# Leaving 384 bytes free under the left side's pools of a one-core hybrid block

## The chip, the cores and the metric

The kernel runs on one core of one Trainium2 chip, in one launch. The metric is the device time of an execution in microseconds (us). Before the change three executions took 1248.18, 1248.79 and 1250.2 us, so the median is 1248.79 us.

Engines are called PE (TensorE; PEld is its weight load), DVE (VectorE), ACT (ScalarE), POOL (GpSimd) and SP (SyncE, which issues most transfers).

## What is computed

One block of a hybrid encoder on x [1, 1024, 1024] in float32. Cut to what matters here:

```
h    = rms_norm(x, pre_mix_gain);  z, xbc, dt, q, k, v = split(h @ w_in)
y_ssd = group_norm(ssd(silu(conv(xbc)), dt) * silu(z))   # 8 heads, chunks
y_sb  = head_norm(stick_breaking_attention(q, k, v))     # 8 heads of 64
x1   = x + rms_norm(concat(y_ssd, y_sb) @ w_out, post_mix_gain)
h2   = rms_norm(x1, pre_ffn_gain)
out  = x1 + rms_norm((silu(h2 @ w_gate) * (h2 @ w_up)) @ w_down, post_ffn_gain)
```

d_model is 1024, the feed-forward width 2816 (22 tiles of 128).

## The kernel before

**Products.** Every large product is made of three: an operand is split into a high and a low part (`split`, L70 to L73: ACT makes the high part, DVE the rest), and `mm3` (L75 to L78) issues high times high, high times low, low times high into one PSUM bank. In a matmul the *stationary* operand (`lhsT`, 128x128 here) is loaded by PEld, and the *moving* operand (`rhs`, 128x512) streams past it. In the profile's names `pd<-folo,fohi` the first name behind the arrow is the moving operand, the second the stationary one; where one name stands, both are tiles of that name.

**Stages.** First in_proj, with attention and SSD interleaved beside it (matmuls `pj_*`, `zp`, `tp`, `o`, `py`), to about 480 us. Then out_proj and the two norms (`po`, `pt`), to about 640 us. Then gate and up as Winograd's seven products per pair of feed-forward tiles (`quad`: `pag`, `pau`, `pbg` .. `peu`): 11 pairs x 2 matrices x 7 products x 12 matmuls = 1848 matmuls of 128x512, to about 1031 us. Then down, again as seven products (`pd`, 924 matmuls), and the last norm.

**Where tiles lie.** On-chip memory (SBUF) is handed out from two ends. Pools with `side="left"` grow upward, pools with `side="right"` grow downward; a pool opened after another was closed takes its place. All addresses below are bytes per partition in the built program. Below the left pools lies `base`, with the identity `ident` (address 16512) and the packed small parameters `pk` (17024, 76 floats). Everything else on the left stands on top of that: `const`, then for the first half `stg`, `att`, `big`, `sml`, `t2`; for the second half `small_p`, `fwA`, `rpA`, `rpB`.

What matters below is where an operand starts within 2048 bytes, since each 128x512 float32 operand is 2048 bytes long, and a 128x128 one 512 bytes:

| operands | pool, side | address modulo 2048 before |
|---|---|---|
| in_proj: `hh`, `hl` moving, `wh_*`, `wl_*` stationary | `hp`, `wp`, right | 2016 (stationary slices at 2016 + 512 i) |
| attention: `kh`, `kl`, `wh`, `wl` moving, `qq`, `vv` stationary | `att`, left | 1984 (+ 512 i) |
| SSD and others in `t2` | left | 256 |
| out_proj: `woh`, `wol` moving | `wo`, right | 2016 |
| out_proj: `yhl` stationary, blocks 2 and 3 (in `rpA`'s places `T3h`, `T3l`, L764) | left | 1632 (+ 512 i) |
| out_proj: `yhl` stationary, the other blocks | `wo`, right | 2016 (+ 512 i) |
| gate and up: `B11`, `B21`, `T2`, `T3`, `T1`, `T4`, `B22` moving | `rpA`, `rpB`, left | 1632 |
| gate and up: first two products' stationary `eo` | `fwA`, left | 1632 (+ 512 i) |
| gate and up: all later stationary `flhi`, `fllo` (`pair`, L936) | `fw`, right | 2016 (+ 512 i) |
| down: `fohi`, `folo`, `doh`, `dol`, both operands | `fw`, `dp`, right | 2016 (+ 512 i) |

So in gate and up the moving operand lies on the left and the stationary one on the right, 384 bytes apart modulo 512; in down both lie on the right, no bytes apart modulo 512. 1848 - 48 = 1800 matmuls of gate and up have `flhi` or `fllo` as stationary operand.

**Order.** Instructions of an engine run in the order in which they stand. PE takes its products one after the other; `pump` and `LOOK` make the left operands of gate and up ahead of their use, `prep` and `AHEAD` those of down.

Of the kernel before, what the change touches and what calls it, by code (L numbers as in the profile page):

```python
# [8 lines left out]
F32 = mybir.dt.float32  # L9
# [4 lines left out]
PSUM = bass.MemoryType.PSUM  # L14
DRAM = bass.MemoryType.DRAM

P = 128
S = 1024
D = 1024
ND = D // P  # L20
NB = S // P
# [13 lines left out]
# what in_proj makes, in order; "ssd" from where on SSD's steps run beside the tiles  # L35
PLAN = ('qkv1', 'x0', 'x1', 'x2', 'x3', 'x4', 'x5', 'qkv2', 'x7', 'x6', 'ssd', 'qkv3', 'z0', 'z1', 'r0', 'z2', 'z3', 'wo', 'l1', 'o0')
# how far attention is where the other stream is 0, 1/8, .. 1 done
# [10 lines left out]
def tile_hybrid_block(  # L48
# [15 lines left out]
    """The rows of x and out run backwards in time (row s is token S-1-s), so that every  # L64
    running product over earlier tokens is a forward scan along the free axis."""
# [4 lines left out]
    def split(hi, lo, src):  # L70
        """hi + lo == src, hi and lo each exact in float32r."""
        A.copy(hi, src)  # L72
        V.tensor_tensor(lo, src, f32(hi), ALU.subtract)  # L73
# [6 lines left out]
    # ------------------------------------------------------------------ constants  # L80
# [11 lines left out]
    make_identity(nc, ident)  # L92
    pk = base.tile([P, 76], F32, name="pk")
# [7 lines left out]
    # TensorE's clock rises with use: products of ones while the first loads run  # L101
# [3 lines left out]
    # tri[s, l] = 1 where s >= l  # L105
    tri = const.tile([P, P], F32, name="tri")
    G.affine_select(tri, ones_f, [[-1, P]], ALU.is_ge, 0.0, base=0, channel_multiplier=1)
    # scan floor: 1 where the key is not strictly before the query, 0 elsewhere
# [3 lines left out]
    # column h is 1 on the 64 partitions of head h of a pair  # L112
# [11 lines left out]
    # DRAM scratch  # L124
# [5 lines left out]
    # means of squares and what they make 1 / rms: even heads, odd heads, SSD groups  # L130
# [8 lines left out]
    # ------------------------------------------------------------------ right side: x * gain and in_proj weights  # L139
# [4 lines left out]
    # the rows' 1 / rms scales columns here, so it is applied to what comes out of in_proj  # L144
# [13 lines left out]
    # sel16 sums the products of the two halves of w2  # L158
# [11 lines left out]
    # columns of w_in in the order of their use; each tile is loaded and split while the one before it  # L170
    # is multiplied
# [5 lines left out]
    def fetch_w(half=None):  # L177
        """The next column tile, or one half of it."""
        if cols:
            name, col = cols[0]  # L180
            w = w_tiles.setdefault(name, [])
            for dh in range(2) if half is None else (half,):
                w.append(load_w_half(col, name, dh))
            if len(w) == 2:
                cols.pop(0)
# [8 lines left out]
    # ------------------------------------------------------------------ pre-mix norm, first products  # L194
# [40 lines left out]
    # ------------------------------------------------------------------ left side: attention, conv and SSD work  # L235
# [20 lines left out]
    def qkv_tiles(j, st):  # L256
        """What takes q, k (each in its two parts) and v of a pair of heads out of PSUM, to DRAM."""

        def store(key, n, i, t):
            nc.sync.dma_start(qkv_d[j][key][i][:, 512 * n : 512 * n + 512], t)  # L260

        def two(key, n, src):
            hi, lo = [t2.tile([P, 512], F32R, tag="t2", name=key + x) for x in "hl"]
            split(hi, lo, src)
            store(key, n, 0, f32(hi))
            store(key, n, 1, f32(lo))

        def evac_q(n, ps, sl):
            two("q", n, ps)
            st["q"] = n == 1  # L270

        def evac_k(n, ps, sl):
            kr = t2.tile([P, 512], F32, tag="t2", name="kr")
            V.tensor_tensor(kr, ps, R_b[:, sl], ALU.mult)
            two("k", n, kr)
            st["k"] = n == 1

        def evac_v(n, ps, sl):
            vr = t2.tile([P, 512], F32, tag="t2", name="vr")
            V.tensor_tensor(vr, ps, R_b[:, sl], ALU.mult)  # L280
            if j == 0:
                v_first.append(vr)
            else:
                store("v", n, 0, vr)
            if n == 1:
                st["v"] = True

        return evac_q, evac_k, evac_v
# [7 lines left out]
    # ------------------------------------------------------------------ dt, decays  # L296
    def dt_stage():
# [18 lines left out]
        # softplus(x) = max(x, 0) + log1p(exp(-|x|)), log1p(e) = 2 atanh(e / (2 + e))  # L316
# [43 lines left out]
        # attention's sigmoids, which need these, wait for the last exponential: ScalarE changes its table once  # L360
# [4 lines left out]
    # ------------------------------------------------------------------ conv tiles  # L365
# [38 lines left out]
    # ------------------------------------------------------------------ SSD  # L404
# [76 lines left out]
    def mean_sq(src, sel, rows, n, cnt, ps=None, start=True, stop=True):  # L481
        """Means of squares over channels, to the rows of ss_d."""
# [32 lines left out]
    # ------------------------------------------------------------------ stick-breaking attention  # L515
    CH = {128: [128], 256: [256], 384: [384], 512: [512], 640: [384, 256], 768: [512, 256], 896: [512, 384], 1024: [512, 512]}

    def prep_head(j, st, h):
        """Keys over both halves of the partitions, the query's high part beside its low part."""
# [29 lines left out]
    def weigh(head, qb):  # L549
        """A key k weighs sigmoid(z_k) * prod_{q < i < k} sigmoid(-z_i)."""  # L550
# [20 lines left out]
    def turn(ws, g, jj):  # L571
        """Weights of 256 queries and 256 keys, keys to the partitions, split."""
# [27 lines left out]
    def attention(st):  # L600
        """All heads, as one stream of small steps: products with the values lag the transposes,
        the next queries' weights run ahead of them."""
# [53 lines left out]
    def merge(ga, gb):  # L656
        """Interleave attention with the other stream, as PACE has it."""
# [47 lines left out]
    # ------------------------------------------------------------------ out_proj: the products  # L705
    # position p of a block of 128 tokens: from here on the last rows come first
# [14 lines left out]
    # the channels in the order of their use: attention's first, the SSD's second group last  # L721
    KO = (4, 5, 6, 7, 0, 1, 2, 3)

    def fetch_wo():
        """W_out's rows in the order of their use, and the places of their two parts."""
# [31 lines left out]
    def out_load(p, part):  # L757
        """A block of the mixed channels, scaled by their 1 / rms, split: all but the SSD's second
        group, that group, or all."""
# [89 lines left out]
    # ------------------------------------------------------------------ out_proj, post-mix norm, residual, pre-ffn norm  # L849
    # positions 0 .. 7 of a block of 128 tokens: from here on the last rows come first  # L850
# [3 lines left out]
    def row_rstd(ssq):  # L854
        """-2 (ssq / D + eps) ** -0.5 for [P, 2] partial sums; the gains it multiplies take in the -1 / 2."""
# [15 lines left out]
    # Gate and up as the seven products of Winograd's form of Strassen's product: blocks of 512  # L871
    # tokens, halves of d, and pairs of tiles of f. h2 is the right operand:
    #   [b11 b12; b21 b22], halves of d by halves of the tokens
# [13 lines left out]
    def product(ps, lop, rop, start):  # L887
        """ps = or += the product; a bank that was read goes on accumulating after that."""
        (ah, al), (bh, bl) = lop, rop
        for k in range(4):  # L890
            mm3(ps, ah[:, k, :], al[:, k, :], bh[:, k, :], bl[:, k, :], start and k == 0, k == 3, not start)
# [4 lines left out]
    def quad(p, name):  # L896
        """The 2 x 2 blocks of W^T h from seven products. c11 is left in PSUM."""
# [35 lines left out]
    def left_gen():  # L933
        """The left operands in the order of their use, gate and up in turn."""
# [51 lines left out]
    def step(p):  # L986
        """The next product of gate's and of up's quad p."""
# [8 lines left out]
    def gate(t):  # L996
        """A block of a from gate's and up's."""
# [8 lines left out]
    # which block of a the products make  # L1006
    where = {1: (0, 0), 4: (1, 1), 5: (1, 0), 6: (0, 1)}

    with es_o:
# [3 lines left out]
        def early_ops():  # L1013
            """The left operands of the first two products."""
# [35 lines left out]
        def out_tail(sb, t):  # L1050
# [20 lines left out]
            # T3 = b22 - b12, T2 = T3 + b11, T1 = b12 - b11, T4 = b21 - T2: its product enters with that sign  # L1071
# [50 lines left out]
        # not the ring's next banks: those hold what waits for the last norm  # L1122
# [7 lines left out]
    # ------------------------------------------------------------------ gate and up  # L1130
# [12 lines left out]
    # Down as seven products too: halves of the tokens, even and odd tiles of f, halves of d.  # L1143
    #   a: [a11 a12; a21 a22], tokens by f; w: [b11 b12; b21 b22], f by d
    # What stays on chip takes the places of what gate and up no longer need, in this order.
# [35 lines left out]
    def prep(i):  # L1181
        """The operands of a step, a product's part of one pair of tiles of f."""
# [60 lines left out]
    # ------------------------------------------------------------------ down, post-ffn norm, residual  # L1243
    dp = ctx.enter_context(tc.tile_pool(reuse_waits="tile", name="dp", bufs=1, side="right"))
    gp_b = gain_b(dp, "gp_b", post_ffn_gain)
    ssq = dp.tile([P, NB, 2], F32, name="ssq")
# [12 lines left out]
    def finish(b, halves, xr):  # L1259
        """halves: the block's two, times the gain."""  # L1260
# [76 lines left out]
def _layout(inputs):  # L1337
    """x backwards in time, plain and transposed; the small parameters side by side, a channel
    (of its tile of 128) to a partition; the large ones as they are."""
# [32 lines left out]
```

## Time and profile before

One execution was profiled. The page gives its span, 1249.6 us from the first to the last instruction; its own time is not listed apart from that. The span lies within the three times that were measured (1248.18 to 1250.2 us).

| stretch, us | PE busy | DVE busy | mean DMA share | what runs |
|---|---|---|---|---|
| 0 to 480 | 457.08 | 388.72 | 0.49 | in_proj, attention, SSD |
| 480 to 640 | 146.00 | 119.62 | 0.72 | out_proj, norms, first products of gate and up |
| 640 to 1210 | 570.00 | 392.32 | 0.34 | gate and up, down |
| 1210 to 1249.6 | 31.16 | 31.44 | 0.60 | the last products and the last norm |

A matmul's recorded duration overlaps the next one's, so a PE row that reads "full" says only that matmuls followed each other without a gap; how fast they followed is read from their starts, or from their number in a stretch.

### The profile page before, as it was taken

How to read it: one execution, taken by the hardware profiler on the slowest of the kernel's cores; microseconds unless marked ns; L12 is line 12 of the kernel's file. 1: busy time of each engine (PE TensorE's matmuls, PEld its weight loads, DVE VectorE, ACT ScalarE, POOL GpSimd, SP SyncE). 2: the span in 40 equal slices, each digit the busy share in tenths (PEclk: the TensorE clock that was granted, in tenths of full speed). 3: DMA queues.
4: the chain of work that ended last, by engine and by line, in shares of the span. 5: the costliest groups of instructions: out<-in, count | busy, mean ns of one | idle time of the engine just before them, and what ended most of it. 6: DMA issues, size and time to landing. Idle time of an engine off the chain costs nothing.

```text
span 1249.6 us, 16320 instructions
## 1 busy us (share of the span) xinstructions
PE 1204.2 (96%) x5641; PEld 972.0 (78%) x5641; DVE 932.1 (75%) x1461; ACT 587.7 (47%) x1115; POOL 92.1 (7%) x232
## 2 busy tenths in 40 slices
PE   8998999999999998998799999999999999999997
PEld 7776778787887776787678888888888888888885
DVE  7478988778997887676897565566555558998777
ACT  7347655556655666444653332333233325444543
POOL 0041110010110100011200000000000000000000
PEclk9998999999999999999899999999999999999999
DMA  5693252445466326754872212312132198133336
GB/s 188 194 358 107 67 152 82 142 117 178 142 181 190 118 93 212 228 173 159 271 207 93 93 60 93 101 59 93 52 100 98 58 327 318 62 124 101 102 135 235
DMA packets 139882, 183.23 MB, mean 147 GB/s; under 512 B 10660, under 2 KB 94852, under 8 KB 139800
## 3 DMA queue, kind: packets, MB, share of 16 engines
q1 hardware_dynamic: 128544, 151.18, 38.3%
q0 software_dynamic: 7424, 25.17, 5.5%
q10 hardware_dynamic: 3832, 5.84, 1.3%
q8 instruction: 44, 0.72, 0.2%
q14 instruction: 38, 0.31, 0.1%
HBM read 132.23 MB, written 49.92 MB: 146 GB/s over the span
## 4 chain that ended last, share of the span: by engine, by line
PE 69%; DVE 14%; DMA 8%; issue 4%; ACT 4%; SPq 2%; DVEq 0%; ACTq 0%
PE pd L77 5%; PE pd L76 5%; PE pd L78 5%; DVE sn L567 3%; DMA Rb<-r_d 3%; PE o L590 2%; PE tp L578 2%; PE pj_x L76 2%; PE pj_x L78 2%; PE pcg L76 2%; PE pj_x L77 2%; PE pcu L76 2%; PE peg L76 2%; PE peu L76 2%; PE peu L77 2%
## 5 line engine op out<-in xcount | busy, mean ns | idle before, releaser
L72 ACT CAST flhi<-fraw 128x512 fp32r<-128x512 f32 x102 | 62.7, 622 | 174.1 <-PE pcg L77 37.0
L77 PE MATMUL pd<-folo,fohi 128*128 128x512 f32 x260 | 101.2, 389 | 0.0
L76 PE MATMUL pd<-fohi 128*128 128x512 f32 x260 | 101.2, 389 | 0.0
L78 PE MATMUL pd<-fohi,folo 128*128 128x512 f32 x260 | 101.1, 389 | 0.0
L567 DVE TENSOR_TENSOR_SCAN sn<-sn,smask 128x1024 f32<-128x1024 f32 (+3 forms) x64 | 87.4, 1366 | 17.7 <-ACT sn L563 17.7
L73 DVE TENSOR_TENSOR fllo<-fraw,flhi 128x512 fp32r<-128x512 f32 x102 | 69.6, 686 | 38.9 <-ACT flhi L72 38.5
L72 ACT CAST fohi<-rt 128x512 fp32r<-128x512 f32 x83 | 48.9, 618 | 51.2 <-PE pd L77 30.7
L563 ACT ACTIVATE sn<-zp,msc 128x512 f32<-128x512 f32 (+2 forms) x96 | 56.0, 585 | 34.3 <-PE zp L562 30.6
L582 ACT CAST wh<-tp 128x512 fp32r<-128x512 f32 (+1 forms) x80 | 42.7, 545 | 38.4 <-PE tp L578 37.9
L72 ACT CAST flhi<-fs 128x512 fp32r<-128x512 f32 x44 | 27.2, 622 | 70.4 <-PE peg L77 37.0
L73 DVE TENSOR_TENSOR folo<-rt,fohi 128x512 fp32r<-128x512 f32 x83 | 55.2, 694 | 6.4 <-ACT fohi L72 6.4
L583 DVE TENSOR_TENSOR wl<-tp,wh 128x512 fp32r<-128x512 f32 (+1 forms) x80 | 49.7, 628 | 10.8 <-ACT wh L582 10.3
L564 ACT ACTIVATE sp<-zp,msc 128x512 f32<-128x512 f32 (+2 forms) x96 | 55.8, 584 | 2.5 <-PE tp L578 2.5
L76 PEld LDWEIGHTS pd<-fohi 128*128 128x128 f32 x260 | 48.8, 188 | 10.3
L78 PEld LDWEIGHTS pd<-fohi,folo 128*128 128x128 f32 x260 | 48.8, 188 | 10.1
L77 PEld LDWEIGHTS pd<-folo,fohi 128*128 128x128 f32 x260 | 48.8, 188 | 10.1
L1004 POOL DMA_DIRECT2D a_d<-sg x44 | 23.7, 540 | 392.4 <-DVE sg L1003 392.4
L76 PE MATMUL pj_x<-hh,wh_x 128*128 128x512 f32 x128 | 52.5, 410 | 0.0
L578 PE MATMUL tp<-ident,sp 128*128 128x128 f32 x288 | 47.6, 276 | 5.0 <-DVE sp L568 4.5
L76 PE MATMUL po<-woh,yhl 128*128 128x512 f32 x128 | 51.0, 399 | 1.0 <-ACT yhl L72 1.0
L78 PE MATMUL po<-woh,yhl 128*128 128x512 f32 x128 | 51.0, 400 | 0.6 <-DVE yhl L73 0.5
L78 PE MATMUL pj_x<-hh,wl_x 128*128 128x512 f32 x128 | 51.1, 399 | 0.0
(422 smaller groups left out, 3479.4 us busy)
## 6 DMA issues: line engine op xcount, KB each, us to landing
ps<-a_d SPq DMA_DIRECT2D x55, 256.0 KB
fraw<-in_w_gate_dram SPq DMA_DIRECT2D x22, 512.0 KB
fraw<-in_w_up_dram SPq DMA_DIRECT2D x22, 512.0 KB
a_d<-sg POOLq DMA_DIRECT2D x44, 256.0 KB, 2.5
rt<-in_w_down_dram SPq DMA_DIRECT2D x33, 256.0 KB
rt<-a_d SPq DMA_DIRECT2D x22, 256.0 KB
ps<-in_w_down_dram SPq DMA_DIRECT2D x22, 256.0 KB
xt<-in_x_t_dram SPq DMA_DIRECT2D x8, 512.0 KB
```

Of the source, the lines that this page charges most:

```text
L72: A.copy(hi, src)
L73: V.tensor_tensor(lo, src, f32(hi), ALU.subtract)
L76: T.matmul(ps, lhsT=ah, rhs=bh, start=start, stop=False, skip_group_check=more)
L77: T.matmul(ps, lhsT=ah, rhs=bl, start=False, stop=False, skip_group_check=more)
L78: T.matmul(ps, lhsT=al, rhs=bh, start=False, stop=stop, skip_group_check=more)
L563: A.activation(sn[:, 1 + off : 1 + off + cw_], zp[:, 0:cw_], AF.Sigmoid, scale=rqn[:, qb : qb + 1])
L564: A.activation(sp[:, off : off + cw_], zp[:, 0:cw_], AF.Sigmoid, scale=rqp[:, qb : qb + 1])
L567: V.tensor_tensor_scan(sn[:, 1 : 1 + W], sn[:, 1 : 1 + W], smask[:, 0:W], 1.0, ALU.mult, ALU.max)
L578: T.transpose(tp[:, P * i : P * i + P], ws[a][:, co : co + P], ident)
L582: A.copy(wh[:, 0:n_], tp[:, 0:n_])
L583: V.tensor_tensor(wl[:, 0:n_], tp[:, 0:n_], f32(wh[:, 0:n_]), ALU.subtract)
L590: T.matmul(o[:, 0:cw_], lhsT=vv[:, k, h, :], rhs=wt[:, c0 : c0 + cw_], start=(first and k == kb + 1 and wt is wh), stop=(last and k == kb ...
```

## The change

An unused tile of 96 floats (384 bytes) is allocated in `base` between `ident` and `pk`. So all that lies on the left above `ident` moves up by 384 bytes: 1632 becomes 2016 in `fwA`, `rpA` and `rpB`, 1984 becomes 320 in `att`, 256 becomes 640 in `t2`. `ident` and all tiles on the right stay. On-chip memory was full but for 320 bytes at down's start, so down's sums of squares `ssq`, 64 bytes on the right, get the first 16 columns of `pk` instead, which held the pre-mix gain and part of the conv weights and aren't read any more by then; `gp_b` moves up by those 64 bytes.

```diff
     ident = base.tile([P, P], F32, name="ident")
     make_identity(nc, ident)
+
+    base.tile([P, 96], F32, name="pad")
     pk = base.tile([P, 76], F32, name="pk")
...
     gp_b = gain_b(dp, "gp_b", post_ffn_gain)
-    ssq = dp.tile([P, NB, 2], F32, name="ssq")
+    ssq = pk[:, 0 : 2 * NB].rearrange("p (b n) -> p b n", n=2)
```

The rest of the diff takes out comments and docstrings.

No instruction is added, removed or moved on any engine, and each waits for the same semaphore values as before. On PE, POOL and SP the rows are the same but for line numbers and buffer numbers; on ACT and DVE the name of one operand is another where down's squares are summed. ACT, near the end of down (`fsc` is the square's unused result, `ssq` its sum, `e` and `y` the first steps of 1 / rms), before:

```order
L1250 ACTIVATE fsc,ssq<-ft 128x512
L72 CAST fohi<-rt 128x512
L857 ACTIVATE e<-ssq 128x1
L858 ACT_TABLE_LOAD
L858 ACTIVATE y_11062<-ssq,e 128x1
```

and the same place in the changed kernel:

```order
L1252 ACTIVATE fsc,pk<-ft 128x512
L72 CAST fohi<-rt 128x512
L859 ACTIVATE e<-pk 128x1
L860 ACT_TABLE_LOAD
L860 ACTIVATE y_11062<-pk,e 128x1
```

Nothing has moved: the sum goes to `pk` instead of `ssq`, two lines further down in the file.

## The prediction, made before the changed kernel was run

> **What bounds the kernel now.** I first read the page's chain of work that ended last, then a table of stretches, then who waited on PE.
>
> ```profile
> span 1249.6 us, 16320 instructions
> PE 69%; DVE 14%; DMA 8%; issue 4%; ACT 4%; SPq 2%; DVEq 0%; ACTq 0%
> ```
>
> The first line is the span, the second the share of each engine in the chain. PE carries it. Where? A table of stretches (busy us and, in brackets, instructions of PE, PEld, DVE, ACT, POOL; then granted clock, DMA share, GB/s):
>
> ```profile
> 0.00:480.00 480.00, 457.08 (x2405) 367.28 (x2406) 388.72 (x534) 277.65 (x519) 53.26 (x160) 0.99 0.49 153
> 480.00:640.00 160.00, 146.00 (x638) 116.84 (x638) 119.62 (x236) 86.25 (x193) 16.15 (x30) 0.96 0.72 224
> 640.00:1030.00 390.00, 390.00 (x1673) 313.76 (x1672) 237.93 (x373) 123.58 (x205) 22.12 (x41) 1.00 0.30 102
> 1035.00:1200.00 165.00, 165.00 (x729) 136.62 (x729) 147.24 (x241) 77.44 (x145) 0.00 (x0) 1.00 0.38 132
> ```
>
> From 640 us (gate and up) to 1200 us (down) PE is busy all the time at a granted clock of 1.00. Its waits from 630 us to the end are two, 0.7 us in total:
>
> ```profile
> PE pcg L76 <- DVE u3g L915: 0.5, 1, 0.5
> PE pd L77 <- DVE dol L73: 0.2, 1, 0.2
> ```
>
> So there the time is the number of matmuls times the step from one start to the next, and a shorter step goes into the time in full. The two rows give that step. All these matmuls are 128x512 in the same three-part form; a stretch counts those that touch it, so I add one duration (0.39 us). Gate and up: 390.39 / 1673 = 233.4 ns. Down: 165.39 / 729 = 226.9 ns. The same work takes **6.5 ns more in gate and up**. What the two stages differ in is where the operands lie: moving left (1632 modulo 2048) against stationary right (2016) in gate and up, both right (2016) in down.
>
> **Is it the offset?** Three places of the same trace separate it from the stage, the line and the side of memory, by the starts of matmuls in the timeline of PE (start, duration, line, output and inputs).
>
> First, the very first products of gate and up have their stationary operand (`eo`) on the left as well, at 1632, beside the same moving `B21`:
>
> ```profile
> 595.87 0.39 PE L76 MATMUL pau<-B21h,eo 128*128 128x512 f32 x1
> ...
> 597.91 0.39 PE L76 MATMUL pau<-B21h,eo 128*128 128x512 f32 x1
> ```
>
> First and last of 10: 2.04 / 9 = 227 ns. Left with left is as quick as right with right. Later in the same loop, with `flhi` on the right:
>
> ```profile
> 800.19 0.40 PE L76 MATMUL pau<-B11h,flhi 128*128 128x512 f32 x1
> 800.43 0.39 PE L77 MATMUL pau<-B11l,flhi 128*128 128x512 f32 x1
> 800.65 0.40 PE L78 MATMUL pau<-B11h,fllo 128*128 128x512 f32 x1
> 800.89 0.39 PE L76 MATMUL pau<-B11h,flhi 128*128 128x512 f32 x1
> 801.12 0.40 PE L77 MATMUL pau<-B11l,flhi 128*128 128x512 f32 x1
> ```
>
> 0.93 / 4 = 233 ns, with longer and shorter steps in turn (0.24 and 0.22 to 0.23).
>
> Second, out_proj, where the moving `woh` is on the right. Blocks 2 and 3 have their stationary `yhl` on the left at 1632, later blocks on the right. First and last of 48 in block 2, and of 42 in a late block:
>
> ```profile
> 510.47 0.40 PE L76 MATMUL po<-woh,yhl 128*128 128x512 f32 x1
> ...
> 521.39 0.39 PE L78 MATMUL po<-woh,yhl 128*128 128x512 f32 x1
> ...
> 582.70 0.39 PE L76 MATMUL po<-woh,yhl 128*128 128x512 f32 x1
> ...
> 592.00 0.39 PE L78 MATMUL po<-woh,yhl 128*128 128x512 f32 x1
> ```
>
> 10.92 / 47 = 232 ns against 9.30 / 41 = 227 ns: the same lines, the same moving tiles, sides swapped, the same cost. Third, in_proj, both on the right; first and last of 15 in one tile's stream:
>
> ```profile
> 60.53 0.40 PE L76 MATMUL pj_q<-hh,wh_q 128*128 128x512 f32 x1
> ...
> 62.60 0.39 PE L76 MATMUL pj_q<-hh,wh_q 128*128 128x512 f32 x1
> ...
> 65.78 0.39 PE L78 MATMUL pj_q<-hh,wl_q 128*128 128x512 f32 x1
> ```
>
> From 62.60 on, 3.18 / 14 = 227 ns; the nine steps before it, just after another kind of matmul had come between, take 2.07 / 9 = 230 ns. So equal offsets settle to 227 after a few matmuls, and offsets 384 bytes apart (modulo 512, the length of a stationary slice) stay at 232 to 233.
>
> **The Trainium skill speaks against this.** "SBUF — State Buffer", section "Who interferes with whom", gives PE two independent read ports, one for the moving operand and one for LDWEIGHTS, and says that PE never waits on anyone. By that page an operand's place would cost nothing, and the change would give 1248.8 us. The rows above differ from it by 5 to 6.5 ns a matmul, so the measurement decides; what the cause inside the memory is, no run here shows.
>
> **The change, part by part.**
>
> *Gate and up.* `B11` and the rest move from 1632 to 2016, the place of `flhi` modulo 2048. The pair then stands as down's does (moving at 2016, stationary slices at 2016 + 512 i), so I take down's step. 1673 matmuls x (233.35 - 226.87) = **10.8 us**, all on PE's stretch without waits. Bounds: 0 (no effect of the offset) and 11.2 (the step of 226.7 that the `eo` rows give). I take 10.8. The 120 or so matmuls with `flhi` ahead of 640 us run between waits for norms and transfers; their 0.8 us I count at nothing, with 0.8 as the other end.
>
> *out_proj, blocks 2 and 3.* 96 matmuls x 5 ns = 0.5 us, but the stretch from 480 to 640 has PE busy 146 of 160 us and waits for transfers and norms. Cover: those waits. I take 0, bounds 0 and 0.5.
>
> *First half.* Pairs on one side move together, so in_proj (right with right) and attention (left with left) keep their distances. New distances arise in three places. Transposes multiply by `ident`, which stays, while their stationary operand moves by 384:
>
> ```profile
> 250.82 0.60 PE L578 MATMUL tp<-ident,sp 128*128 128x128 f32 x4
> 521.63 1.03 PE L1061 MATMUL pt<-ident,tm 128*128 128x128 f32 x8
> ```
>
> `sp` stands at 384, `tm` at 96 modulo 512, `ident` at 128. With a last duration of 0.27 us, the steps are 0.33 / 3 = 0.11 and 0.76 / 7 = 0.11 us: no dependence at two quite different distances, so 0. The 32 matmuls of dt are left with right before and after: at most 32 x 5 ns = 0.2 us either way. And at the borders between in_proj's stream and attention's the distance goes from 32 to 160 bytes modulo 512. No row shows that case; one bound is 0, the other is the rival below. I take 0, since streams are unsettled after a border today as well (60.53 to 62.60).
>
> *`ssq` in `pk`.* No wait is added. 16 squares and their readers write and read another place. The nearest rows are DVE's, with one input on the left and all on the right:
>
> ```profile
> L73 DVE TENSOR_TENSOR folo<-rt,fohi 128x512 fp32r<-128x512 f32 x83 | 55.2, 694 | 6.4 <-ACT fohi L72 6.4
> L73 DVE TENSOR_TENSOR folo<-ps,fohi 128x512 fp32r<-128x512 f32 x37 | 25.6, 692 | 11.1 <-ACT fohi L72 11.0
> ```
>
> 694 against 692 ns: 2 ns an instruction either way, under 0.1 us. I take 0. The same rows say that DVE doesn't gain from the new places.
>
> *What is late next?* Between 640 and 1030 us DVE is busy 238 of 390 us, ACT 124, DMA 0.30: none is near PE. Where gate and up end, transfers are dense, and then DVE is full:
>
> ```profile
> 1015.00:1055.00 40.00, 40.00 (x176) 32.70 (x175) 27.87 (x46) 16.68 (x29) 1.62 (x3) 1.00 0.99 363
> 1055.00:1075.00 20.00, 20.00 (x90) 16.56 (x89) 20.00 (x35) 10.30 (x19) 0.00 (x0) 1.00 0.20 74
> ```
>
> The loads start on events of PE and so come earlier with it; only from 1015 to 1030 does PE gain on them, 15 x 6.5 / 233 = 0.4 us, against 0.2 us of PE's waits in all of down. I take 0, bounds 0 and 1.1 us lost (the whole last pair, 39 us, at the same rate).
>
> Sum: span 1249.6 - 10.8 = 1238.8 us. The span is 0.8 above the median of the runs, so the time is 1248.79 - 10.8 = **1238.0 us**.
>
> **Rivals.**
>
> *A, the offset isn't the cause.* Left against right could cost by itself, as two parts of the memory, whatever the offset; then the change does nothing: 1248.8 us. For it: in each slow pair the operands are on different sides, and no row has left and right at one offset. Against it: distance in the memory doesn't order the rows.
>
> ```profile
> L77 PE MATMUL peg<-T1l,flhi 128*128 128x512 f32 x44 | 17.4, 395 | 0.0
> L77 PE MATMUL pd<-folo,fohi 128*128 128x512 f32 x260 | 101.2, 389 | 0.0
> ```
>
> `T1l` (address 140896) is 31 KB below `flhi` (172000) and slow (395 ns), `folo` is 20 KB above `fohi` and quick (389 ns), and in_proj's `hh` and `wh`, settled at 227, are up to 80 KB apart. 8 in 100. The Trainium skill's page named above comes to the same time by another way, no cost of place at all.
>
> *B, given back behind gate and up.* The saturated transfers, or DVE, hold down's start: 1.1 us lost as above, 1239.1 us. PE's waits there, 0.2 us, speak against it. 7 in 100.
>
> *C, the first half loses its near alignment.* in_proj's stream (2016) and attention's (1984) lie 32 bytes apart now, 160 after. If the stationary load of the next matmul meets the moving operand of the one before it, each border disturbs the stream more, and in_proj's 24 x 2 x 24 = 1152 matmuls settle less often. At gate and up's step that costs 1152 x 6.5 = 7.5 us, so 1245.5 us; at the longer of its two steps in turn (0.24) 1152 x 13 = 15 us, so 1253 us. It makes the kernel slower from 10.8 us / 1152 = 9.4 ns each. PE is busy 457 of 480 us there, so it would be felt. Against it: within a stream, the pairs are unchanged, and the rows from 62.60 on settle after any border. 2 in 100 for slower; 5 in 100 for a loss of 2 to 8 us, 1240 to 1246 us.
>
> **How the numbers follow.** The forecast as it stands has 78 in 100, between 1235.5 us (with 0.8, 0.5 and 0.4 us of the gains that I counted at nothing, and the 0.6 us between the median and the lowest run) and 1239.5 us (the 1.4 us between the median and the highest run). The range takes in B and the mild end of C besides: 1235.5 to 1241.5 us; that leaves out A and the dear part of C. A measurement of this kernel can tell 0.2%, 2.5 us, from no change. Faster by more: the forecast, B and most of the mild C, 0.89. Within: A, mostly, 0.08. Slower: C's dear end, 0.03.
>
> **What would show it.** In the changed profile the recorded step of gate and up should be 227 ns, 390 us of it shrink to 379, with 222 matmuls in 50 us as in down; blocks 2 and 3 of out_proj should step at 227; in_proj, transposes and down should be as they are; the stretch up to 640 us should end within 1 us of where it does now. A step that stays at 233 is A; a PE wait of over 0.5 us between 1020 and 1060 us is B; `pj` steps above 230 in long streams are C.

## The result and the profile after

| kernel | median, us | runs | lowest to highest, us | ratio to before, 95% interval |
|---|---|---|---|---|
| before | 1249.13 | 4 | 1248.18 to 1250.2 | |
| changed | 1241.33 | 4 | 1240.09 to 1242.37 | 0.9933 [0.9919, 0.9947] |

The changed kernel is faster by 7.8 us (medians). That is inside the range 1235.5 to 1241.5, near its upper end and 3.3 us above the 1238.0 forecast. It lies outside 1235.5 to 1239.5, where the prediction put its plain forecast. So the direction holds, and the size has to be explained. Of two kernels below one run each is left out, 1480.39 and 1691.89 us at granted clocks of 0.75 and 0.65 against about 0.99 in all others.

The profiled execution of the changed kernel took 1240.09 us, 1.7 us more than its span. It is the quickest of its four runs. In every run on record the time is 1.7 to 1.8 us longer than the span. So the profiled execution of the kernel before, whose span alone is 1249.6 us, took about 1251.3 us (an estimate), longer than each of its four timed runs; what stands ahead compares that span with times as if they were the same. The 10.8 us of the prediction don't depend on it. The two profiles are therefore 11.2 us apart, where the medians are 7.8 us apart. First, its page (the span; the shares of the chain of work that ended last):

```profile
span 1238.4 us, 16320 instructions
...
PE 70%; DVE 11%; issue 8%; DMA 5%; ACT 4%; SPq 1%; POOL 1%; DVEq 0%; ACTq 0%; POOLq 0%
```

PE still carries the chain. Then the table of stretches for the same kernel (columns as in the prediction):

```profile
0.00:480.00 480.00, 457.81 (x2412) 367.39 (x2413) 389.07 (x535) 278.11 (x520) 53.41 (x160) 1.00 0.50 154
480.00:640.00 160.00, 145.08 (x633) 116.70 (x632) 120.03 (x237) 85.61 (x193) 16.15 (x30) 0.95 0.72 222
...
640.00:1020.00 380.00, 380.00 (x1675) 314.75 (x1674) 236.25 (x371) 123.18 (x205) 22.13 (x41) 1.00 0.33 104
1025.00:1190.00 165.00, 165.00 (x730) 136.71 (x729) 147.43 (x242) 77.39 (x144) 0.00 (x0) 1.00 0.39 135
```

The first two stretches and down (730 matmuls in 165 us, 729 before) are nearly as they were. Gate and up now pass 1675 matmuls in 380 us; before, 1673 took 390. The step is best read in a stretch well inside the stage. PE alone, before and then changed (busy us, matmuls, clock, DMA share, GB/s):

```profile
660.00:1010.00 350.00, 350.00 (x1502) 1.00 0.26 86
```

```profile
660.00:1010.00 350.00, 350.00 (x1546) 1.00 0.30 94
```

350.39 / 1502 = 233.3 ns before, 350.39 / 1546 = 226.6 ns after: gate and up now step as down does.

Where, then, are the missing microseconds? PE's waits from 620 us on, changed kernel (us in all, times, longest):

```profile
PE pcg L76 <- DVE u3g L917: 2.1, 1, 2.1
```

That wait was 0.5 us before. The same 14 us in both kernels, before first:

```profile
632.00:646.00 14.00, 13.52 (x59) 10.65 (x58) 13.39 (x23) 6.74 (x12) 0.12 (x1) 1.00 0.63 178
```

```profile
632.00:646.00 14.00, 11.91 (x46) 9.37 (x45) 13.58 (x23) 7.08 (x13) 0.54 (x1) 0.88 0.56 162
```

13 matmuls fewer, and a granted clock of 0.88 in place of 1.00. The timeline of PE in the changed kernel shows both losses in turn (start, duration, and in brackets the idle time ahead and what ended it):

```profile
635.42 0.39 PE L78 MATMUL peu<-T1h,fllo 128*128 128x512 f32 x1
637.90 0.59 PE L76 MATMUL pcg<-T4h,flhi 128*128 128x512 f32 x1 [2.09 <-DVE u3g L917]
638.29 0.63 PE L77 MATMUL pcg<-T4l,flhi 128*128 128x512 f32 x1
638.72 0.63 PE L78 MATMUL pcg<-T4h,fllo 128*128 128x512 f32 x1
...
641.27 0.51 PE L78 MATMUL pcg<-T4h,fllo 128*128 128x512 f32 x1
641.62 0.39 PE L76 MATMUL pcg<-T4h,flhi 128*128 128x512 f32 x1
641.85 0.39 PE L77 MATMUL pcg<-T4l,flhi 128*128 128x512 f32 x1
```

After the idle 2.09 us the step is 0.43 us for seven steps (2.98 / 7), and soon 0.23 again. The stretch of it in the table has the clock at one half:

```profile
638.20:641.40 3.20, 3.20 (x9) 2.44 (x8) 3.20 (x7) 1.22 (x2) 0.00 (x0) 0.50 0.14 45
```

Why does `u3g` come late? DVE's timeline of the changed kernel:

```profile
633.84 1.52 DVE L73 TENSOR_TENSOR B22l<-B22l,B22h 128x512 fp32r<-128x512 f32 x2 [0.29 <-ACT B22h L72]
635.27 0.68 DVE L911 TENSOR_TENSOR p1u<-pbu,p1u 128x512 f32<-128x512 f32 x1
635.87 1.28 DVE L73 TENSOR_TENSOR B22l<-B22l,B22h 128x512 fp32r<-128x512 f32 x2
637.07 0.68 DVE L917 TENSOR_TENSOR u3g<-pcg,p1g 128x512 f32<-128x512 f32 x1
```

`u3g` reads the bank `pcg`, and the product with `T4` accumulates on that bank afterwards, so PE has to wait for the read. In DVE's order `u3g` stands behind the four splits of `B22`, whose input comes back from memory just then and whose result PE needs only after all of `T4`.

For a comparison that doesn't hang on where a window is cut, I took the starts of the same matmuls, counted in PE's order, in several profiled executions (us from one start to the next; "again" is the changed kernel profiled twice more, "B22 later" is told below):

| from, to | matmuls | before | changed | again, 1 | again, 2 | B22 later | before, B22 later |
|---|---|---|---|---|---|---|---|
| start, to the first `o` behind the last `tp` | 2411 | 480.69 | 479.82 | 481.98 | 479.95 | 479.79 | 482.65 |
| to the first `pag` with `flhi` | 498 | 118.70 | 117.56 | 121.01 | 121.41 | 119.07 | 120.76 |
| to the last `pcu` with `T3` | 103 | 33.27 | 32.52 | 32.20 | 32.47 | 33.38 | 32.04 |
| to the second `peg` with `B22` | 50 | 12.37 | 15.37 | 15.35 | 15.01 | 11.34 | 12.54 |
| to the last of gate and up | 1654 | 385.93 | 374.91 | 374.90 | 374.91 | 374.92 | 384.35 |
| most of down | 846 | 191.78 | 191.76 | 191.76 | 191.76 | 191.76 | 191.77 |
| the rest | | 26.88 | 26.43 | 27.25 | 27.43 | 27.43 | 27.22 |

Before to changed, with a sign: -0.9, -1.1, -0.8, **+3.0**, **-11.0**, 0, -0.5, in all -11.2 us of span. The first two rows scatter by 2.9 and 3.9 us among these executions, the same kernel (changed and its two repeats) by 2.2 and 3.9 of them, so the 2.0 us gained there in this pair can't be put down to the change. The -11.0 and the +3.0 are what is left to test.

### The profile page after: what moved, and what is told of

Its sections match the earlier page's. It is cut to its first block, busy times and chain, and to the rows that moved or that the text cites. A ratio compares the mean times of both kernels' runs of the same rounds, so it can differ in the third digit from the quotient of the medians.

```text
span 1238.4 us, 16320 instructions
## 1 busy us (share of the span) xinstructions
PE 1192.9 (96%) x5641; PEld 972.5 (79%) x5641; DVE 931.1 (75%) x1461; ACT 587.2 (47%) x1115; POOL 92.2 (7%) x232
## 4 chain that ended last, share of the span: by engine, by line
PE 70%; DVE 11%; issue 8%; DMA 5%; ACT 4%; SPq 1%; POOL 1%; DVEq 0%; ACTq 0%; POOLq 0%
PE pd L76 5%; PE pd L78 5%; PE pd L77 5%; DVE sn L569 3%; PE o L592 2%; PE tp L580 2%; PE pj_x L76 2%; PE pj_x L78 2%; PE pcg L76 2%; PE pj_x L77 2%; PE pcg L77 2%; PE pcg L78 2%; PE pcu L77 2%; PE peu L77 2%; PE peg L77 2%
## 5 line engine op out<-in xcount | busy, mean ns | idle before, releaser
L585 DVE TENSOR_TENSOR wl<-tp,wh 128x512 fp32r<-128x512 f32 (+1 forms) x80 | 49.6, 628 | 10.8 <-ACT wh L584 10.2
L77 PEld LDWEIGHTS pd<-folo,fohi 128*128 128x128 f32 x260 | 48.8, 188 | 10.1
L76 PEld LDWEIGHTS pd<-fohi 128*128 128x128 f32 x260 | 48.8, 188 | 10.1
```

The costliest lines, as they stand in the source:

```text
L76: T.matmul(ps, lhsT=ah, rhs=bh, start=start, stop=False, skip_group_check=more)
L77: T.matmul(ps, lhsT=ah, rhs=bl, start=False, stop=False, skip_group_check=more)
L585: V.tensor_tensor(wl[:, 0:n_], tp[:, 0:n_], f32(wh[:, 0:n_]), ALU.subtract)
```

## The experiments

Run beside them, the kernel before had medians of 1249.64 us (17 runs; the first four experiments), 1248.17 (one run; both sides, 128, 256, 352 bytes) and 1251.91 us (17 runs; the last four). Ratios below are to those.

**The changed kernel once more.**

> The changed kernel once more, for the size: the matmul steps of gate and up account for 10.8 us, four runs showed 7.8 (6.6 to 10.1). Theory O (the offset between the two operands of a matmul sets its step, nothing else changed): 9 to 11 us below before, gate and up at 227 ns a matmul. Theory C (the first half gives 2 to 3 us back, because its left pools now lie 160 instead of 32 bytes from the right's): 7 to 8.5 us below, the first 480 us longer by 2 to 3 us in the trace.

1242.96 us (6 runs, 1239.99 to 1246.16), ratio 0.9936 [0.9919, 0.9953]. The profiled execution was the longest one. Its column in the table has the same 374.91 and nearly the same 15.35. Gain and loss repeat; what makes it longer is in the rows that scatter anyhow. The median lies 6.7 us below before, less than either theory expected, and the first 480 us (481.98 in the table) are no longer than in the executions of before's first half (479.1 to 482.7, with `ssq` alone and with the splits later).

**The free bytes only from out_proj on**, so that the whole first half lies as before:

```diff
-    base.tile([P, 96], F32, name="pad")
...
+    pad_p = ctx.enter_context(tc.tile_pool(..., name="pad_p", bufs=1, side="left"))
+    pad_p.tile([P, 96], F32, name="pad")
```

> The 384 bytes are left free only from out_proj on, so the first half lies as in the kernel before. O: the same time as the changed kernel within 1 us, gate and up at 227 ns. C: 2 to 3 us faster than the changed kernel, since the first half keeps its 32 bytes of distance.

1240.62 us (5 runs, 1239.41 to 1241.69), ratio 0.9925 [0.991, 0.9939]. Gate and up take 374.91 us from the `B22` product on. So the whole gain is there without any move in the first half. The median is 2.3 us below that of the changed kernel, as much as theory C expected, but the intervals overlap, and in the profiles the difference doesn't lie in the first half: the mean of in_proj's (`pj`) steps under 0.26 us is 229.16 ns in the changed kernel, 229.38 here, 229.34 before. It lies at the place of the 50 matmuls around 640 us, 12.49 us here (taken as in the table) against 15.0 to 15.4.

**Only `ssq` in `pk`, no free bytes.**

> Only the move of the sums of squares into pk, without the free bytes. O: the time of before within 1 us, gate and up at 233 ns. A rival by which the move of the sums costs the missing 2 to 3 us: 1251 to 1252 us, the last 40 us longer.

1249.45 us (12 runs), ratio 1.0 [0.9988, 1.0011]: that part is worth nothing. But one look at its step shows something that the prediction didn't have:

```profile
660.00:1010.00 350.00, 350.00 (x1508) 1.00 0.28 88
```

350.39 / 1508 = 232.4 ns, with the same offsets as before (233.3). Its starts repeat 230, 232, 241, 232, 231, 232, 228 and so on, where before had 229 and 238 in turn. **Operands at unequal offsets settle into one of at least two rhythms**, 384.4 or 385.9 us for the 1654 matmuls; of three profiled executions with 384 bytes between them, one (before) is in the second.

**Two parts of free bytes**, 32 in `base` and 352 from out_proj on, which also puts attention's operands at in_proj's offset:

```diff
-    base.tile([P, 96], F32, name="pad")
+    base.tile([P, 8], F32, name="pad0")
...
+    pad_p.tile([P, 88], F32, name="pad")
```

> 32 bytes free in the first half and 352 more from out_proj on: attention's pools lie exactly at in_proj's offset (0 bytes instead of 32), the second half as in the changed kernel. O: as the changed kernel, within 1 us, or up to 2 us faster if streams settle sooner after a border. C: 3 us or more faster than the changed kernel, in_proj's mean step under 229 ns.

1240.65 us (5 runs, 1237.12 to 1241.59), ratio 0.9921 [0.9904, 0.9937]. No gain over the late free bytes that can be measured; of this kernel only the times are used.

**Both sides moved**: 256 bytes free on the left and 128 on the right, so that both operands start at 1888.

```diff
-    base.tile([P, 96], F32, name="pad")
+    base.tile([P, 64], F32, name="pad")
...
+    pad_r = ctx.enter_context(tc.tile_pool(..., name="pad_r", bufs=1, side="right"))
+    pad_r.tile([P, 32], F32, name="padr")
```

> 256 bytes free under the left side's pools and 128 above the right side's, so that the second half's operands of both sides lie at 1888 modulo 2048. Theory O (the distance between the two operands sets the step): 226.7 ns a matmul in gate and up, as in the changed kernel. Rival A (it is the place 2016 of the moving operand that counts): 232 to 234 ns.

1242.21 us (one run). Gate and up:

```profile
660.00:1010.00 350.00, 350.00 (x1546) 1.00 0.29 94
```

As quick as the changed kernel, at another address. So at these two addresses the distance counts, not the place.

**128, 256 and 352 bytes free instead of 384** (`[P, 32]`, `[P, 64]`, `[P, 88]`). The operands are then 256, 128 and 32 bytes apart.

> 128 bytes free instead of 384: moving at 1760, stationary at 2016 + 512 i, 256 bytes apart modulo 512. O with a period of 512 or more: 230 ns or more in gate and up. O with a period of 256: 226.7 ns.

> 256 bytes free: moving at 1888, stationary at 2016 + 512 i, 128 bytes apart modulo 512. O with a period of 512 or more: 228 to 234 ns. O with a period of 128: 226.7, but then the kernel before, 384 bytes apart, would have been quick too.

> 352 bytes free: moving at 1984, stationary at 2016 + 512 i, 32 bytes apart, which is the distance between attention and in_proj in the first half of before. O, if only equality counts: 230 ns or more. O, if nearness counts: 226.7 to 228 ns.

The stretch in the three, in this order:

```profile
660.00:1010.00 350.00, 350.00 (x1546) 1.00 0.29 94
```

```profile
660.00:1010.00 350.00, 350.00 (x1501) 1.00 0.26 86
```

```profile
660.00:1010.00 350.00, 350.00 (x1501) 1.00 0.27 87
```

1242.4, 1252.06 and 1253.62 us (one run each). 256 bytes apart is as quick as equal offsets (226.6 ns); 128 and 32 bytes apart are as slow as 384 (233.4 ns). **Of the distances tried, 0 and 256 are quick, 32, 128 and 384 slow**: what fits all of them is a period of 256 bytes, not of 512 or 2048, and no gradual dependence on nearness. The prediction's `eo` rows (both operands at 1632, 227 ns) fit too. With 256 bytes free the moving operand starts at 1888, as with both sides moved; there the stationary one starts at 1888 as well and the step is quick, here at 2016 and it is slow. So it isn't the moving operand's place alone.

**The wait at 640 us.** The theory, called W: the quicker step lets PE come early to the `T4` product, where it waits for `u3g`; the idle time is followed by half clock; together they give back 3 us of the gain. Three of the runs so far fit it badly: with 256 and 352 bytes free the step is slow and the wait is still 1.2 and 1.7 us, and with the late free bytes the step is quick and the wait only 0.9:

```profile
PE pcg L76 <- DVE u3g L917: 1.2, 1, 1.2
PE pcg L76 <- DVE u3g L917: 1.7, 1, 1.7
PE pcg L76 <- DVE u3g L918: 0.9, 1, 0.9
```

The time of the 50 matmuls there, taken as in the table, says so too. With the slow step it is 12.37 us (before), 12.38 (`ssq` alone), 13.12 (256 bytes) and 13.65 (352 bytes); with the quick step 15.37, 15.35 and 15.01 (changed), 12.49 (late), 13.81 (both sides) and 15.27 (128 bytes). The two sets overlap, and their means are 1.7 us apart, not 3. So it had to be tried. The splits of `B22` can be done later, since only the product after `T4` reads them. Here they come behind `u3g` and `u3u` on DVE, and their ACT halves move with them; PE's order stays:

```diff
             nc.sync.dma_start(f32(lo), late_d[i][c])
-            split(hi, lo, f32(lo))
+            if i < 2:
+                split(hi, lo, f32(lo))
...
             gate(step(p))
+            if p == 0 and done[0] == 4:
+                for c in range(4):
+                    hi, lo = [x[:, :, P * c : P * c + P] for x in B22]
+                    split(hi, lo, f32(lo))
```

Put into the changed kernel (column "B22 later" of the table):

> The changed kernel, with B22's four splits moved on DVE from ahead of u3g to behind the first pair's products; PE's order is as before. Theory W (the changed kernel gives back about 2 to 3 us at 640 us, because PE now comes early to the T4 product and waits 2.1 us for u3g, which stands on DVE behind splits that wait for a load; the idle time is followed by a stretch at half clock): PE's wait for u3g under 0.5 us, no half-clock stretch near 640 us, and 1.5 to 3 us less than the changed kernel run beside it, so 1238.5 to 1241 us. Rival (the wait only moves to the next product that needs a late load, or it is hidden anyway): within 1 us of the changed kernel.

Into the kernel before:

> The kernel before with the same splits moved, nothing else. Theory W: before waits only 0.5 us for u3g and has no half-clock stretch there, so it gains under 1 us: 1248.5 to 1249.6 us. Rival (moving the splits is worth 2 to 3 us by itself, whatever the offset): 1246 to 1247.5 us.

Into the kernel before with 128 bytes free and `ssq` where it was:

> The kernel before with 128 bytes left free instead of 384 (operands of gate and up 256 bytes apart modulo 512), down's sums of squares left in their own tile, and the splits moved. If the step depends on the distance modulo 256: step 226.7 ns in gate and up, and within 1 us of the 384-byte kernel with the splits moved. If 256 bytes apart costs something that one look could not show: 1 us slower or more.

And the changed kernel on the same chip:

> The changed kernel once more, for comparison on the same chip: 1240.5 to 1243.5 us, with a wait for u3g of about 2 us near 640 us.

| kernel | median, us | runs | lowest to highest, us | ratio to before, 95% interval |
|---|---|---|---|---|
| changed, again | 1241.83 | 6 | 1241.15 to 1244.65 | 0.9921 [0.9906, 0.9936] |
| changed, B22 later | 1239.74 | 5 | 1239.44 to 1242.12 | 0.9911 [0.9895, 0.9927] |
| 128 bytes, B22 later | 1240.23 | 6 | 1238.61 to 1243.05 | 0.9912 [0.9895, 0.9928] |
| before, B22 later | 1248.85 | 12 | 1247.4 to 1253.05 | 0.998 [0.9969, 0.9991] |

In the changed kernel with the splits later, PE's timeline at the same place and DVE's beside it:

```profile
637.68 0.39 PE L78 MATMUL peu<-T1h,fllo 128*128 128x512 f32 x1
637.91 0.39 PE L76 MATMUL pcg<-T4h,flhi 128*128 128x512 f32 x1
638.13 0.39 PE L77 MATMUL pcg<-T4l,flhi 128*128 128x512 f32 x1
```

```profile
634.96 0.68 DVE L917 TENSOR_TENSOR u3g<-pcg,p1g 128x512 f32<-128x512 f32 x1
635.56 0.68 DVE L917 TENSOR_TENSOR u3u<-pcu,p1u 128x512 f32<-128x512 f32 x1
636.15 1.28 DVE L73 TENSOR_TENSOR B22l<-B22l,B22h 128x512 fp32r<-128x512 f32 x2
```

and its 14 us:

```profile
632.00:646.00 14.00, 14.00 (x63) 11.54 (x62) 13.25 (x22) 7.19 (x13) 0.00 (x0) 1.00 0.62 175
```

The row of the table goes from 15.37, 15.35 and 15.01 to 11.34 us: order on DVE was the cause of the wait, and without the idle time there is no half clock here. All three profiled kernels with the splits later have no wait of the `T4` product for `u3g`, the ten others, with the splits in their old place, have one of 0.5 to 2.1 us. So much is shown: **about 3.7 to 4.0 us lie at this place in the changed kernel's profiled executions.** In whole runs it is less clear. The medians differ by 2.1 us, as W expected, but the two intervals overlap widely. And the kernel before gains 0.2% as well (3.1 us between medians), where W gave under 1 us, although its row for this place (12.54 against 12.37) shows no gain. (Its 1248.85 us alone would lie in W's range, but the kernel before beside it ran at 1251.91.) So the rival of that run, that the later splits are worth 2 to 3 us whatever the offset, isn't refuted, and W as a theory of the *difference* between the two kernels isn't carried by the times. With the splits later in both, the change is worth 0.9911 / 0.998 = 0.993, no more than without (0.9921 here, 0.9933 at first). One candidate wasn't tried: the kernel before with the splits later was in the 232.4 ns rhythm, the profiled execution of before in the other, 1.6 us longer. What chooses the rhythm, and how often before runs in each, these profiles can't tell, as there is one of each of these kernels.

The kernel with 128 bytes free and the splits later comes within 0.5 us of the one with 384, so `ssq` needn't move; its 1654 matmuls of gate and up take 374.93 us, as with equal offsets. These two have the lowest medians of the four, though their intervals overlap with the changed kernel's.

## Why the prediction was right, and where its size was off

The mechanism that it named is the one that works, and that the kernel gets faster is no luck. That the number lies in the range is partly luck. The plain forecast ended at 1239.5 us; from there to 1241.5 the range held room for rival B and the mild end of rival C, and what was lost, so far as it is known, was lost by neither of them. (The four amounts named for the lower end add up to 2.3 us, which gives 1235.7 and not 1235.5; nothing hangs on it.)

- **What bounds the kernel: right.** Gate and up are PE without waits, and the step went into that stage's time in full: 226.6 ns, in all quick kernels alike.
- **Is it the offset: right in kind, too narrow in its rule.** It is the distance between moving and stationary operand, but, by the distances tried, modulo 256, not modulo 512 as the prediction wrote. The runs at other distances show it; the change itself couldn't.
- **Gate and up, 10.8 us: the rate was right for this one execution, and mis-sized as a typical one.** From the first `B22` product on, the saving is 11.0 us against the profiled execution of before, and 9.5 us against the profiled execution of `ssq` alone, which has the same offsets. The term took one execution's rhythm for the kernel's. No run was profiled often enough to say which is typical.
- **The matmuls ahead of 640 us, counted at nothing with a gain as the other end: the bound left out a loss.** "The stretch up to 640 us should end within 1 us of where it does now", said the prediction. In the one pair it did, at 645.0 and 645.3 us, but by chance: the 2.8 us that PE came earlier, 2.0 of them in the rows that scatter, were given back in the next 50 matmuls. In three of three profiled executions of the changed kernel these take 15.0 to 15.4 us, in the profiled one of before 12.4: 2.6 to 3.0 us lost against it, from a wait of 1.8 to 2.1 us (0.5 before) and a stretch at half clock. Against all the profiled executions with the slow step it is less, 1.7 us between the means. The prediction quoted the row of that wait and didn't ask what holds `u3g` up. 9.5 to 11.0 less 2.6 to 3.0 is 6.5 to 8.4 us, and the medians of the changed kernel lie 7.8, 6.7 and 10.1 us below before. That these are the whole of the 3.3 us missing from the forecast fits the first two, but isn't shown: the interval of each ratio is 3.5 us or more wide, and that of the third (8.0 to 11.8 us) holds the 10.8 us as well.
- **out_proj, blocks 2 and 3: right.** Their step went from 232.4 and 232.5 ns to 226.7 and 226.9, that of all blocks from 228.7 to 227.0 (steps under 0.25 us), and the time isn't found again in the row of this stretch, which scatters by 3.9 us.
- **First half, transposes, `ssq`, down: right.** `pj` steps 229.2 against 229.3 ns, `tp` 109 ns in both (median); `ssq` alone 1.0; down 191.8 us in all kernels.
- **Rival A, the side and not the offset: fell.** Left and right at one offset are quick, at two different addresses (2016 and 1888), and left and right 256 bytes apart are quick too.
- **Rival B, given back behind gate and up: fell in its place.** No wait of PE over 0.2 us there. A loss of its kind came ahead of the stage instead, by a wait for DVE.
- **Rival C, the first half loses: fell.** The mean step of `pj` is 229.2 ns in the changed kernel and 229.3 before. The late free bytes, which spare the first half, gain 2.3 us more by the medians, but within the intervals and, in the profile, at another place.
- **The Trainium skill's rule** ("SBUF — State Buffer", "Who interferes with whom"), two independent read ports and no waiting: the row and the runs go against it, 226.6 against 232.4 to 233.4 ns a matmul by the distance alone. What inside the memory or PE makes the difference stays open.

## What to carry to other kernels

Where PE runs without gaps and each matmul loads a new stationary operand, compare the step of stages with the same shapes; if they differ by a few per cent, look at the start addresses of the two operands modulo 256, and free a few bytes below one of them. Before counting a faster stage in full, look at the waits where it begins: a wait of half a microsecond says that the other engine is just about even, and here its order (what stood ahead that wasn't needed yet) decided how long PE waited. One profiled execution gives one rhythm; take the term from two executions, where it carries the sum.

## What the runs showed of the hardware that was not expected

- The step of a 128x512 matmul with a stationary load each time: 226.6 ns at distances of 0 and 256 bytes, 232.4 to 233.4 at 32, 128 and 384. The slow case has rhythms, 229 and 238 in turn, a longer one with a 241, or (at 32 bytes) 232 and 235 in turn, and the mean step of each held through the stage's 1654 matmuls once settled.
- An idle time of PE of about 2 us was enough for half clock: in five profiled executions with a wait of 1.8 us or more at `u3g`, four had some 3 us at a granted clock of 0.50 behind it (the fifth, with both sides moved, and those with waits of 0.5 to 1.7 us had none). It costs 1.4 us here, on top of the 2.1 of the wait. The Trainium skill ("TensorE: Matmul & The Clock Gate", "Why this matters for your kernels") warns of gaps above about 3 us; here the measured 1.8 to 2.1 us count.
